# A decoder layer's opening: x's first half loaded early, memory's squares summed by additions, two inverse roots by square root

## The chip, the cores and the metric

The kernel runs on one core of one Trainium2 chip. The metric is the device time of one execution in microseconds; 2423.27 us is the median of the runs before the change.

## The reference

The reference is one layer of a hybrid decoder on 1024 tokens of width 1024. Only its opening matters here.

```python
def rms_norm(x, g):
    xf = x.astype(jnp.float32)
    y = xf * lax.rsqrt(jnp.mean(xf * xf, axis=-1, keepdims=True) + NORM_EPS)
    return (y * g.astype(jnp.float32)).astype(x.dtype)

def swiglu(u, w_in, w_out):
    gate, up = jnp.split(u @ w_in, 2, axis=-1)
    return (jax.nn.silu(gate) * up) @ w_out

# in the layer:
f1 = swiglu(rms_norm(h, ffn1_pre_g[l]), ffn1_w_in[l], ffn1_w_out[l])
...
mem_n = rms_norm(mem, mem_norm_g[l])          # mem: 256 tokens, used by the cross-attention
km, vm = jnp.split(mem_n @ w_kv, 2, axis=-1)  # needs only mem: no result of the layer
```

The rest of the layer (a recurrent branch, a windowed attention, the cross-attention into `mem`, a gated merge and a second SwiGLU) comes after both and is not touched.

## The kernel before

**Layout.** Activations lie feature-major: a tile holds 128 features by 512 tokens. x is 8 feature tiles by two halves of the tokens, `x[k][h]`, 256 KB each; `mem_x` is one tile of 8 by 256 columns. Each float32 operand of a product is split into a rounded part (`hi`, a cast on ACT, L126 for weights, L240 for activations) and a rest (`lo`, a subtraction on DVE, L128 and L241), and a product takes three matmuls, hi by hi, hi by lo, lo by hi (`mm3`, L190 to L192).

**Weights.** They come in strips of 512 KB in one fixed order (`plan`): four strips of memory's key projection (`mkv_k`), four of its value projection (`mkv_v`), then the first feed-forward layer (`ffn1_gate` and so on). `raw` (L113) issues a strip's load on SP's queue into one of two buffers (`RAWS = 2`), so that a third strip's load waits until the first strip has been split. `prefetch` (L155) keeps eight split operands (four strips) ready; it runs inside `take`, before each use. For the `mkv` strips POOL makes the second half's subtraction.

**Order.** The program is written in one order, and a scheduler puts each engine's instructions into theirs: an instruction has the number of its place in the program, and of those that are ready the lowest number goes first. `high_priority(offset=n)` lowers the numbers inside it by n: `lead` is 300, `urgent` is 1000. Each engine then runs its list strictly in order, SP's DMA issues too.

**The opening** (`build`, L1198 to L1205). Memory's two loads are written (`memory_load`, L818), then x's sixteen (L1201), then `memory_kv` (L823), `factors_norm` of x's first half (L288) and `factors_first` (L296).

- `memory_kv`: `mem_hi` and `mem_lo`, memory times its gains, split (L830 on ACT, L831 on DVE). Two halves of squares on ACT (L835, one buffer), each summed over its four feature tiles by one DVE reduction (L837). `rstd` turns the sums into inverse roots. The four `mkv_k` strips are multiplied into four PSUM banks (`pq`); each bank is emptied by L849, which multiplies with the inverse roots (`mem_rs`). The bank tag has four buffers, so `mkv_v`'s two banks wait for L849. Then the four `mkv_v` strips.
- `factors_norm`: squares of the eight x tiles (ACT, L250), seven additions (DVE, L254), `rstd`, then eight multiplications in place (DVE, L294). `factors_first` splits the eight tiles (L240, L241); the first feed-forward products (`px`, `py`) need them.
- `rstd` (L211): matmuls with a column of ones sum over features (`ps_ms`, L218); on DVE, with two or four columns, a scale (L221), a first guess by shifting the bits (L226, L227), and three Newton steps of three instructions (L230 to L232); four matmuls spread the result over the partitions (`ps_rs`, L236). With `quick` the guess is DVE's reciprocal and ScalarE's square root (L223, L224) and one Newton step; before the change only the kernel's last norm, into the output, uses it.

After the opening the feed-forward layer takes nine strips with x's first half alone, while x's second half is loaded, normalized and combined (`factors_part`, `factors_end`), and then goes on with both.

Of the kernel before, what the change touches and what calls it, by code (L numbers as in the profile page):

```python
# [10 lines left out]
F32 = mybir.dt.float32  # L11
F32R = mybir.dt.float32r
I32 = mybir.dt.int32
ALU = mybir.AluOpType
ACT = mybir.ActivationFunctionType
AXX = mybir.AxisListType.X

P = 128
T = 1024
TH = 512  # L20
D = 1024
KD = D // P
DFF = 2816
KF = DFF // P
MEM = 256
# [6 lines left out]
HALVES = ((0, 0, TH), (1, 0, TH))  # L32
# [5 lines left out]
KH = KD // 2  # L38
# [37 lines left out]
class Builder:  # L76
# [208 lines left out]
            self.nc.scalar.copy(raw[:, 8 + h * TH : 8 + (h + 1) * TH], o)  # L285


    def factors_norm(self, xs, part, gname, pool):  # L288

        h, lo, hi = part  # L290
        xs = [x[h][:, lo:hi] for x in xs]
        rs = self.rstd([self.sum_squares(xs, pool)], D, pool, hi - lo)[:, : hi - lo]
        for k in (0, 4, 1, 5, 2, 6, 3, 7):
            self.nc.vector.scalar_tensor_tensor(xs[k], xs[k], self.vec(gname, k), rs, ALU.mult, ALU.mult)  # L294

# [17 lines left out]
    def quarters(self, xs):  # L313
        return ([xs[k + a][h] for k in range(KH)] for h in (0, 1) for a in (0, KH))
# [508 lines left out]
    def memory_kv(self, pool, km_d, vm_d):  # L823
        nc, x = self.nc, self.mem_x
        V = nc.vector
        hi = pool.tile([P, KD, MEM], F32R, name="mem_hi", bufs=1)
        lo = pool.tile([P, KD, MEM], F32R, name="mem_lo", bufs=1)
        for k in range(KD):
            g = self.vec("mem_norm_g", k)
            nc.scalar.activation(hi[:, k], x[:, k], ACT.Copy, scale=g)  # L830
            V.scalar_tensor_tensor(lo[:, k], x[:, k], g, hi[:, k].bitcast(F32), ALU.mult, ALU.subtract)  # L831
        parts = []
        for a in (0, KH):
            sq = pool.tile([P, KH, MEM], F32, tag="mem_sq", name="mem_sq", bufs=1)
            nc.scalar.activation(sq, x[:, a : a + KH], ACT.Square)  # L835
            s = pool.tile([P, MEM], F32, tag="mem_ss", name="mem_ss", bufs=2)
            V.tensor_reduce(s, sq.rearrange("p k t -> p t k"), AXX, ALU.add)  # L837
            parts.append(s)

        ps, col = self.rstd(parts, D, pool, MEM, True)  # L840
        rs = pool.tile([P, MEM], F32, name="mem_rs", bufs=1)
        nc.scalar.copy(rs, ps[:, :MEM])
        for h in range(4):
            w = self.strip("mkv_k", h)
            ps = self.psum("pq")
            for k in range(KD):
                self.mm3(ps[:, :MEM], self.block(w, k), (hi[:, k], lo[:, k]), k == 0, k == KD - 1)
            t = pool.tile([P, MEM], F32, tag="km", name="km", bufs=2)
            V.tensor_tensor(t, ps[:, :MEM], rs, ALU.mult)  # L849
            nc.scalar.dma_start(km_d[:, h], t)  # L850
        pv = [self.psum("pq") for _ in (0, 1)]
        for s in range(4):
            w = [tuple(x.rearrange("p b c -> p (b c)") for x in op) for op in self.strip("mkv_v", s)]
            for a in (0, 1):
                k = 2 * s + a
                for i in (0, 1):
                    cols = slice(i * P, (i + 1) * P)
                    self.mm3(pv[i], (hi[:, k, cols], lo[:, k, cols]), w[a], k == 0, k == KD - 1)
        for i in (0, 1):
            t = pool.tile([P, 512], F32, tag="vm", name="vm", bufs=2)  # L860
            nc.scalar.activation(t, pv[i], ACT.Copy, scale=col[:, i : i + 1])
            nc.scalar.dma_start(vm_d[:, i], t)
# [303 lines left out]
    def build(self):  # L1166
        nc, tc, io = self.nc, self.tc, self.io
        with contextlib.ExitStack() as outer, tc.tile_pool(reuse_waits="tile", name="consts", bufs=1) as cp, \
# [26 lines left out]
            with quarters() as self.qpool:  # L1195
                x = self.acc_tiles()
                with tc.tile_pool(reuse_waits="tile", name="start", bufs=1) as pool:
                    self.memory_load(pool)  # L1198
                    for h in (0, 1):
                        for k in range(KD):  # L1200
                            nc.sync.dma_start(x[k][h], io["xT"][:, k, h * TH : (h + 1) * TH])  # L1201
                    self.memory_kv(pool, km_d, vm_d)
                    self.factors_norm(x, HALVES[0], "ffn1_pre_g", pool)
                    self.factors_first(x)
                self.ffn_in("ffn1", x, hid_d, first_d, HALVES[1:], lambda part, pool: self.factors_norm(x, part, "ffn1_pre_g", pool))  # L1205
                consts, raws = contextlib.ExitStack(), contextlib.ExitStack()
                mixc = consts.enter_context(tc.tile_pool(reuse_waits="tile", name="mixc", bufs=1))
                self.rawpool = raws.enter_context(tc.tile_pool(reuse_waits="tile", name="raws", bufs=len(MIX_FIRST)))
                self.mixer_consts(mixc)
                with tc.tile_pool(reuse_waits="tile", name="ffn_out", bufs=2) as pool:  # L1210
                    acc = self.acc_tiles()
                    for part in self.ffn_outs("ffn1", hid_d, acc, HALVES):
                        xr = self.residual(io["xT"], part, self.res_tile)
                        self.post_norm(acc, part, lambda k: self.post1[:, k : k + 1], xr, pool, h1)
                        self.pre_norm(acc, part, "mix_pre_g", u, pool)
                    self.mixer_first(u, pool, att_d)
            mixed = self.mixer(u, mixc, raws.close, att_d, gate_d, km_d, vm_d)
            consts.close()
            with quarters() as self.qpool:
                merged = self.last_branches(*mixed)  # L1220
                x = self.acc_tiles()
                projection = self.out_projection(merged, x)
                post = lambda part, xr, pool: self.post_norm(x, part, lambda k: self.vec("mix_post_g", k), xr, pool, h2)
                part = next(projection)
# [91 lines left out]
```

## Time and profile before

| | us |
|---|---|
| median of 3 runs (2422.99 to 2425.74) | 2423.27 |
| the profiled execution | 2416.87 |
| its span, first to last instruction | 2415.2 |
| PE busy in the span | 2356.7 |
| DVE busy | 1570.0 |
| ACT busy | 915.2 |
| first product matmul starts, after the span's start | 8.32 |
| first feed-forward matmul starts | 43.81 |

Times inside the execution are counted from the span's start. The profiled execution lies 6.4 us under the median and 1.67 us over its span. PE is TensorE's matmuls, PEld its weight loads, DVE is VectorE, ACT ScalarE, POOL GpSimd, SP the queue that issues most loads (SPq in a row is such an issue, whose duration is that of the issue and not of the transfer). A matmul's duration overlaps its neighbours'; the distance between the starts of two is what one costs.

### The profile page before, as it was taken

The page shows a single profiled execution, that of the slowest core. Times are in us where ns is not written, and L with a number is a line of the kernel's source. Part 1 is how long each engine was busy: PE and PEld are TensorE (multiplying, and loading weights), DVE is VectorE, ACT ScalarE, POOL GpSimd, SP SyncE. Part 2 cuts the span into 40 slices and gives each one's busy share as a digit, 9 for nine tenths or more (in the row PEclk, how much of TensorE's full clock was granted, in tenths as well). Part 3 has the DMA queues.
Part 4 walks back from the last instruction along what each step waited for, and adds up shares of the span by engine and source line. Part 5 has one row for each costly group of instructions (what it writes and reads, how often), then busy time and mean ns, then how long its engine had stood idle before and what let it go on. Part 6 is the DMA issues. An engine that isn't in the chain of part 4 may idle for free.

```text
span 2415.2 us, 33278 instructions
## 1 busy us (share of the span) xinstructions
PE 2356.7 (98%) x12500; PEld 1917.6 (79%) x12500; DVE 1570.0 (65%) x2598; ACT 915.2 (38%) x1712; POOL 105.0 (4%) x142
## 2 busy tenths in 40 slices
PE   7999999999999999999999999999999999999997
PEld 6788888788888777887777877778888778878887
DVE  7976555654488775993435367675988665564457
ACT  6523333422345533222334454334652223342143
POOL 1000000000000000001210000240000000000000
PEclk9999999999999999999999999999999999999999
DMA  7453222532244245225326434454545432253235
GB/s 246 156 187 114 89 86 79 177 117 99 101 157 141 103 149 183 97 96 184 125 78 203 129 114 144 165 181 160 176 162 175 148 127 80 90 197 105 79 112 190
DMA packets 161921, 332.16 MB, mean 138 GB/s; under 512 B 31552, under 2 KB 61760, under 8 KB 161504
## 3 DMA queue, kind: packets, MB, share of 16 engines
q1 hardware_dynamic: 146304, 302.70, 37.1%
q10 hardware_dynamic: 15456, 27.33, 3.2%
q8 instruction: 98, 1.61, 0.3%
q14 instruction: 63, 0.52, 0.1%
HBM read 239.80 MB, written 89.13 MB: 136 GB/s over the span
## 4 chain that ended last, share of the span: by engine, by line
PE 79%; DVE 10%; DMA 5%; ACT 3%; issue 3%; POOL 0%; ACTq 0%; SPq 0%; DVEq 0%; POOLq 0%
PE po L190 6%; PE po L191 6%; PE po L192 6%; PE px L190 5%; PE px L191 5%; PE px L192 5%; PE pgate L190 4%; PE pgate L192 3%; PE pgate L191 3%; PE pz L191 2%; PE pz L192 2%; PE pz L190 2%; DVE w_lo L128 2%; DMA w_raw<-in_ffn_in 2%; PE pr L192 2%
## 5 line engine op out<-in xcount | busy, mean ns | idle before, releaser
L126 ACT CAST w_hi<-w_raw 128x512 fp32r<-128x512 f32 x592 | 363.0, 620 | 883.1 <-PE po L191 260.6
L128 DVE TENSOR_TENSOR w_lo<-w_raw,w_hi 128x512 fp32r<-128x512 f32 x584 | 408.6, 703 | 173.1 <-ACT w_hi L126 166.4
L190 PE MATMUL po<-u,w_hi 128*128 128x512 f32 (+1 forms) x768 | 286.7, 373 | 2.2 <-DVE acc L472 2.2
L192 PE MATMUL po<-u,w_lo 128*128 128x512 f32 (+1 forms) x768 | 286.1, 373 | 0.0
L191 PE MATMUL po<-u,w_hi 128*128 128x512 f32 (+1 forms) x768 | 286.0, 372 | 0.0
L475 DVE TENSOR_TENSOR acc<-po,acc 128x512 f32<-128x512 f32 (+1 forms) x136 | 89.5, 658 | 154.4 <-PE po L192 154.1
L190 PEld LDWEIGHTS po<-u,w_hi 128*128 128x128 f32 x768 | 145.4, 189 | 28.1 <-DVE acc L472 3.4
L192 PEld LDWEIGHTS po<-u,w_lo 128*128 128x128 f32 x768 | 145.5, 189 | 25.1
L191 PEld LDWEIGHTS po<-u,w_hi 128*128 128x128 f32 x768 | 145.4, 189 | 24.8
L190 PE MATMUL pgate<-u,w_hi 128*128 128x512 f32 x384 | 154.2, 402 | 0.0
L192 PE MATMUL pgate<-u,w_lo 128*128 128x512 f32 x384 | 153.7, 400 | 0.0
L191 PE MATMUL pgate<-u,w_hi 128*128 128x512 f32 x384 | 153.0, 399 | 0.0
L190 PE MATMUL px<-f,w_hi 128*128 128x512 f32 x352 | 137.9, 392 | 6.2 <-DVE u L396 4.2
L191 PE MATMUL px<-u,w_hi 128*128 128x512 f32 x352 | 137.3, 390 | 0.6 <-DVE u L241 0.6
L191 PE MATMUL pz<-u,w_hi 128*128 128x512 f32 x352 | 136.9, 389 | 0.3 <-DVE u L241 0.3
L190 PE MATMUL px<-u,w_hi 128*128 128x512 f32 x352 | 136.9, 389 | 0.3 <-ACT u L240 0.3
L192 PE MATMUL px<-u,w_lo 128*128 128x512 f32 x352 | 137.2, 390 | 0.0
L191 PE MATMUL px<-f,w_hi 128*128 128x512 f32 x352 | 137.1, 389 | 0.0
L192 PE MATMUL px<-f,w_lo 128*128 128x512 f32 x352 | 137.1, 389 | 0.0
L192 PE MATMUL pz<-u,w_lo 128*128 128x512 f32 x352 | 136.9, 389 | 0.0
L190 PE MATMUL pz<-u,w_hi 128*128 128x512 f32 x352 | 136.9, 389 | 0.0
L192 PE MATMUL pr<-u,w_lo 128*128 128x512 f32 x224 | 89.1, 398 | 0.0
(324 smaller groups left out, 4679.2 us busy)
## 6 DMA issues: line engine op xcount, KB each, us to landing
w_raw<-in_ffn_in SPq DMA_DIRECT2D x110, 512.0 KB
w_raw<-in_ffn_out SPq DMA_DIRECT2D x68, 512.0 KB
w_raw<-in_win SPq DMA_DIRECT2D x56, 512.0 KB
hid_d<-g SPq DMA_DIRECT2D x88, 256.0 KB
hid<-hid_d SPq DMA_DIRECT2D x88, 256.0 KB
gate_d<-gate SPq DMA_DIRECT2D x24, 512.0 KB
pk_d<-pk ACTq DMA_DIRECT2D x4, 2560.0 KB
f<-pk_d SPq DMA_DIRECT2D x16, 640.0 KB
```

The source lines that it names most:

```text
L126: self.nc.scalar.copy(hi, x)
L128: (engine or self.nc.vector).tensor_tensor(lo, x, hi.bitcast(F32), ALU.subtract)
L190: mm(out, wh, xh, start=first, stop=False, **kw)
L191: mm(out, wh, xl, start=False, stop=False, **kw)
L192: mm(out, wl, xh, start=False, stop=last, **kw)
L475: self.nc.vector.tensor_tensor(out, ps, out, ALU.add)
```

## The change

`rstd`'s `quick` is handed through `factors_norm`; the function itself is as before. `prefetch` is called ahead of everything else, x's first half is loaded with numbers lowered by 1000, and x's second half is loaded after `memory_kv` in the program. Memory's two halves of squares get a buffer each; one addition of 128x1024 adds them, and two more (128x512 and 128x256) fold the four tiles that are left, so that `ps_ms` takes one operand in place of two.

```diff
-    def factors_norm(self, xs, part, gname, pool):
+    def factors_norm(self, xs, part, gname, pool, quick=False):
...
-        rs = self.rstd([self.sum_squares(xs, pool)], D, pool, hi - lo)[:, : hi - lo]
+        rs = self.rstd([self.sum_squares(xs, pool)], D, pool, hi - lo, quick=quick)[:, : hi - lo]
...
-        parts = []
+        sqs = []
         for a in (0, KH):
-            sq = pool.tile([P, KH, MEM], F32, tag="mem_sq", name="mem_sq", bufs=1)
+            sq = pool.tile([P, KH, MEM], F32, tag="mem_sq", name="mem_sq", bufs=2)
             nc.scalar.activation(sq, x[:, a : a + KH], ACT.Square)
-            s = pool.tile([P, MEM], F32, tag="mem_ss", name="mem_ss", bufs=2)
-            V.tensor_reduce(s, sq.rearrange("p k t -> p t k"), AXX, ALU.add)
-            parts.append(s)
-
-        ps, col = self.rstd(parts, D, pool, MEM, True)
+            sqs.append(sq)
+        s = sqs[0]
+        V.tensor_tensor(s, s, sqs[1], ALU.add)
+        for n in (2, 1):
+            V.tensor_tensor(s[:, :n], s[:, :n], s[:, n : 2 * n], ALU.add)
+
+        ps, col = self.rstd([s[:, 0]], D, pool, MEM, True, quick=True)
...
+                    self.prefetch()
                     self.memory_load(pool)
-                    for h in (0, 1):
-                        for k in range(KD):
-                            nc.sync.dma_start(x[k][h], io["xT"][:, k, h * TH : (h + 1) * TH])
+                    load = lambda h: [nc.sync.dma_start(x[k][h], io["xT"][:, k, h * TH : (h + 1) * TH]) for k in range(KD)]
+                    with tc.high_priority(offset=self.urgent):
+                        load(0)
                     self.memory_kv(pool, km_d, vm_d)
-                    self.factors_norm(x, HALVES[0], "ffn1_pre_g", pool)
+                    load(1)
+                    self.factors_norm(x, HALVES[0], "ffn1_pre_g", pool, quick=True)
```

## Rows read from the trace of the kernel before

**Rows 1.** The page, busy time of each engine (us, share of the span, instructions)

```profile
PE 2356.7 (98%) x12500; PEld 1917.6 (79%) x12500; DVE 1570.0 (65%) x2598; ACT 915.2 (38%) x1712; POOL 105.0 (4%) x142
```

**Rows 2.** Busy time by stretches: PE, PEld, DVE, ACT, POOL, granted clock, DMA share, GB/s

```profile
8.00:14.00 6.00, 5.68 (x25) 5.49 (x26) 5.38 (x10) 5.56 (x12) 1.04 (x2) 1.00 1.01 383
27.90:34.50 6.60, 6.60 (x20) 5.54 (x21) 4.67 (x17) 1.88 (x4) 2.54 (x2) 0.50 0.84 277
43.80:48.70 4.90, 3.67 (x14) 1.94 (x12) 4.41 (x8) 3.70 (x8) 0.00 (x0) 1.00 0.73 222
70.00:100.00 30.00, 30.00 (x134) 24.84 (x133) 29.05 (x48) 15.67 (x28) 0.00 (x0) 1.00 0.50 167
```

**Rows 3.** PE in order of time: start, duration, line, operation, idle before and its releaser

```profile
8.32 0.79 PE L190 MATMUL pq<-mem_hi,w_hi 128*128 128x256 f32 x2 [8.32 <-ACT mem_hi L830]
...
26.49 0.71 PE L236 MATMUL ps_rs<-ident,rsy 128*128 128x128 f32 x4 [2.44 <-DVE rsy L232]
27.89 1.87 PE L218 MATMUL ps_ms<-ones,sq 128*128 128x1 f32 x8 [0.69 <-DVE sq L254]
...
31.04 0.63 PE L190 MATMUL pq<-w_hi,mem_hi 128*128 128x512 f32 x1
31.47 0.63 PE L191 MATMUL pq<-w_lo,mem_hi 128*128 128x512 f32 x1
...
34.96 1.05 PE L236 MATMUL ps_rs<-ident,rsy 128*128 128x128 f32 x8
...
43.81 0.39 PE L190 MATMUL px<-u,w_hi 128*128 128x512 f32 x1
44.04 0.39 PE L190 MATMUL py<-r,w_hi 128*128 128x512 f32 x1
...
62.29 1.02 PE L218 MATMUL ps_ms<-ones,sq 128*128 128x1 f32 x8 [1.08 <-DVE sq L254]
...
104.60 0.50 PE L191 MATMUL pz<-u,w_hi 128*128 128x512 f32 x1 [0.34 <-DVE u L241]
```

**Rows 4.** SP's queue in order of time, its first issues

```profile
0.81 0.87 SPq L119 DMA_DIRECT2D w_raw<-in_mkv_k  x2
1.73 0.90 SPq L821 DMA_DIRECT2D mem_x<-in_memT  x2
2.67 1.06 SPq L1201 DMA_DIRECT2D acc<-in_xT  x2
7.03 2.00 SPq L119 DMA_DIRECT2D w_raw<-in_mkv_k  x2
```

**Rows 5.** The chain of waits in order of time: start, length, what

```profile
1.73 5.95 DMA mem_x<-in_memT
```

**Rows 6.** DVE in order of time, memory's squares and inverse root

```profile
15.40 2.03 DVE L837 TENSOR_REDUCE mem_ss<-mem_sq 128x256 f32<-128x1024 f32 x1
...
18.35 0.16 DVE L221 TENSOR_SCALAR rsm<-ps_ms 128x2 f32<-128x2 f32 x1 [0.26 <-PE ps_ms L218]
...
21.29 1.26 DVE L231 TENSOR_TENSOR rsq<-rsq,rsh 128x2 f32<-128x2 f32 x1
...
22.86 0.68 DVE L254 TENSOR_TENSOR sq<-sq 128x512 f32<-128x512 f32 x1
...
26.27 0.16 DVE L232 SCALAR_TENSOR_TENSOR rsy<-rsq,rsy 128x2 f32<-128x2 f32 x1
```

**Rows 7.** POOL in order of time

```profile
16.24 1.29 POOL L128 TENSOR_TENSOR w_lo<-w_raw,w_hi 128x512 fp32r<-128x512 f32 x1 [1.31 <-ACT w_hi L126]
20.88 1.66 POOL L128 TENSOR_TENSOR w_lo<-w_raw,w_hi 128x512 fp32r<-128x512 f32 x1 [3.34 <-ACT w_hi L126]
```

**Rows 8.** The kernel's end, ACT's table load, then the chain of waits

```profile
2352.56 1.28 ACT L224 ACT_TABLE_LOAD   x1
...
2404.99 0.17 DVE rsm L221
...
2406.01 0.17 DVE rsy L232
```

## The prediction, made before the changed kernel was run

> **What bounds the kernel now.** The page's busy times come first [rows 1]: PE is busy 2356.7 of 2415.2 us, no other engine over 65%. So the kernel is as long as TensorE's work plus the time in which TensorE stands still or runs slowly, and an opening can give only the second kind. The busy times by stretches show where in the opening that is [rows 2]: 27.9 to 34.5 us runs at a granted clock of 0.50, and from 43.8 to 48.7 us PE is busy for 3.67 of 4.90 us. PE in order of time names the waits [rows 3]. It starts at 8.32 us, when memory's first split tile is there; it waits 2.44 us for memory's inverse roots (the `mkv_v` products need a PSUM bank, a bank is emptied by L849, and L849 needs the roots); then 0.69 us for the sum of x's squares; and it comes back to the `mkv_v` products at half clock, 0.43 us from one matmul to the next against 0.23 us for the same width at 43.81. The chain of waits begins with memory's own load, 1.73 to 7.68 us [rows 5]. So early on two things bound: when memory arrives, and DVE's chain from memory and x to their roots. Later there is a second bound: from 70 to 100 us DVE is busy 29.05 of 30 us, and at 104.60 a matmul waits 0.34 us for DVE's split of x's second half [rows 2, 3]. What the opening gains must be gained on DVE too, or it is lost there.
>
> **x's loads.** The code lowers their numbers by 1000, the weights' by 300. That numbers decide, and not the place in the program, is seen on SP's queue: the first two strips are written after memory and x, and are issued first, at 0.81, with memory at 1.73 and x at 2.67 [rows 4]. The third strip waits for its buffer until 7.03. Ahead of it now stand all eight x tiles, which is what the change says. But memory's loads have no lowered number, so I take it that x goes ahead of memory as well (and probably of the first two strips, which changes nothing in the sum). That is 8 tiles of 256 KB, 2.10 MB. When the queues are full the transfers run at 383 GB/s from 8 to 14 us [rows 2], so memory lands 5.5 us later, near 13.2 us, and PE's first product starts near 13.8. Cost: **+5.5**. The other end is 0, memory still first. SP's issues themselves cost little: two x issues took 1.06 us [rows 4], eight take 4.2, inside that time. Third and fourth strip come about 3 us later than now, behind 1.05 MB of memory; PE has two strips to work on by then, and I cost them at 0. If that cover is gone, it is at most the same 5.5.
>
> **What then leaves PE's path.** (a) x's sum and root. x is in by about 8 us (5.5 us of transfer from 2.7 on), its squares need ACT and DVE, which have little else to do before memory comes; so `ps_ms` (1.87 us) and `ps_rs` (1.05 us) [rows 3] run while PE has nothing to do: **-2.9**. The wait of 0.69 goes with them: **-0.7**. (b) Memory's root. Today it takes from 18.35 to 26.43 (26.27 and 0.16), 8.1 us, since its 12 small instructions after L221 stand between 0.68 us additions and w_lo subtractions on DVE, and one of them took 1.26 us [rows 6]. The quick form stands at the kernel's end: from L221 to the last step 1.2 us where nothing lies between [rows 8]. In company I take 3 us; the bounds are 1.2 and 8.1. The squares' sums cost two reductions of 2.03 us [rows 6]; the three additions, by 0.68 for 512 columns, 1.4 + 0.7 + 0.4 = 2.5 us, so 1.5 us less. The chain from memory's landing to the roots was 26.43 - 7.68 = 18.75 us and becomes about 12; PE asks for the roots at 26.49 - 2.44 = 24.05, 15.7 us after its start, and so finds them with 3 us to spare: **-2.4**. (c) One operand in place of two in `ps_ms` takes out two of its four products; I take **-0.4** (0 to 0.9, from half of 1.87). (d) Without the idle time ahead of them, the `mkv_v` products run at full clock. From 29.6 to 34.5 us 12 of them came 0.43 apart in place of 0.23: **-2.4**, or 0 if the clock falls all the same. (e) From 43.8 to 48.7 us 14 matmuls need 3.2 us at 0.23 and take 4.9; they wait for splits of x [rows 2, 3] which DVE will have made: **-1.7**, or 0 where the splits stay last. (f) The wait of 1.08 us ahead of the second half's `ps_ms` at 62.29 goes in part: **-0.5** (0 to -1.1).
>
> ScalarE gets two square roots and at most one more load of its tables, 1.28 us at the kernel's end [rows 8]; both lie in the 3 us to spare in (b). x's second half is now written after `memory_kv`, as filler for SP behind the strips; its sum is asked for only at 62.29 [rows 3], and nine strips of the first half alone cover it: 0, or a later wait there if it lands late.
>
> Sum: +5.5 - 2.9 - 0.7 - 2.4 - 0.4 - 2.4 - 1.7 - 0.5 = **-5.5 us**. On DVE the same stretch loses 1.5 us of sums, seven small instructions of 0.16 us in each of two roots (2.2), and some of the waits like that of 1.26 us (three L231 took 1.2 us or more; one shows in rows 6): 3.7 to 7 us; and it has idle time to give, 1.9 us in 27.9 to 34.5 alone. So DVE can just follow by 5.5 us and the gain can be kept. Against the profiled execution, 2416.87 us, this gives 2411.4; the median stands 6.4 above that execution, so the forecast is 2423.27 - 5.5, or **2417.8**.
>
> **A rule against it.** Memory's reduction at 15.40 took 2.03 us although POOL's subtraction ran from 16.24 to 17.53 beside it; L231, with two operands in SBUF, began at 21.29 inside POOL's 20.88 to 22.54 and ended with it [rows 6, 7]. The additions have two such operands, so by POOL's durations one of them can wait 0 to 1.7 us. Two such waits, 3.4 us, would use up the 3 us to spare in (b) and cost PE 0.4: a sum of -5.1 in place of -5.5, or 2418.2. I take none, since POOL works less than half of that stretch. The Trainium skill's page "SBUF — State Buffer" (Who interferes with whom) has it as a rule: a DVE instruction with two SBUF inputs and a GpSimd one that reads SBUF block each other whole, and a reduction never contends. The trace agrees.
>
> **The rivals.** *Memory is not behind x* (SP takes the strips and memory first, as the words "ahead of the third strip" may mean). For it: that is what they say; against it: the numbers. Then the +5.5 falls away, but x's matmuls stay on the path, +2.9, and DVE, which could follow by 7 to 9 at most, bounds: about -8.5, **2414.8**. *The gain is given back*: the opening is shorter, but DVE at 100 us has not followed, or the strips' loads come late. For it: DVE is full in that stretch; against it: its removed work. By DVE's lower figure, 3.7, less one POOL wait of 1.7, the gain is about 2: **2421.3**. *Memory's late arrival decides*: the stretch from memory to the first feed-forward product keeps its length, because L849 still waits for the roots behind DVE's x work (eight multiplications and seven additions now stand ready just when memory comes), PE idles and the clock falls as before. Then only the +5.5 is left: **2428.8**, slower. It decides if the wait ahead of `ps_rs` stays over 2 us; against it is that the small root's instructions are fewer and go first by number. The half-way case, stalls half gone, lies within 0.2%.
>
> **The numbers.** 0.2% is 4.85 us, about what a measurement can tell. Chances: the forecast 0.50, its own range 2415.5 to 2420.0; memory first 0.15; given back 0.23; memory late 0.12. Faster by over 0.2% (under 2418.4) is memory first and seven tenths of the forecast's own range, 0.51; within 0.2% is the rest of it and the gain given back, 0.37; slower is 0.12. The range from 2413.8 to 2425.5 leaves out most of the slower case and the best of memory first.
>
> **What would show it.** On SP's queue eight x issues before memory's, memory landing near 13 us and the first product near 13.8; x's `ps_ms` and `ps_rs` before that product; no wait over 0.5 us ahead of memory's `ps_rs`; a granted clock of 1.00 through the `mkv_v` products; the first feed-forward product near 40 us with no gaps after it; and the strips after 100 us still some 5 us earlier. A wait of 2 us or more for roots, a clock of 0.50 after it, or a wait at x's second half that grows by what the opening gained would prove the sum wrong, each at its own term.

## The result: slower by a quarter of a per cent

The changed kernel took 2432.94 us (median of 15 runs, 2429.27 to 2436.60), the kernel before beside it 2427.17 us (15 runs): a ratio of 1.0026, with a 95% interval of [1.0018, 1.0035]. Run a second time (after_again, below), the change gave 1.0036 [1.0024, 1.0048]. That is slower by more than the 0.2% that the prediction took for measurable (the lower end of the first interval lies a little under it), where it had forecast 5.5 us faster.

| | before, us | after, us |
|---|---|---|
| profiled execution | 2416.87 | 2429.78 |
| its span | 2415.2 | 2428.1 |
| first product matmul starts | 8.32 | 14.20 |
| memory's `ps_rs` starts | 26.49 | 29.69 |
| first `mkv_v` matmul starts | 29.62 | 31.68 |
| x's `ps_ms` starts | 27.89 | 42.59 |
| first feed-forward matmul starts | 43.81 | 50.85 |
| first store of a hidden tile (L415) | 124.21 | 132.07 |

The spans differ by 12.9 us, the medians by 5.8. A second profile of the kernel before, below, has a span of 2422.2 with an opening like the first one's; so two profiles of one kernel differ by 7 us, and only the opening is compared row by row here, never the two spans.

The page's busy times after answer to [rows 1]: PE is as busy as before, within 1.0 us, so the time that was added is time in which PE stands still.

```profile
PE 2357.7 (97%) x12496; PEld 1918.5 (79%) x12496; DVE 1564.8 (64%) x2585; ACT 917.2 (38%) x1715; POOL 107.5 (4%) x142
```

SP's queue after, in order of time, against [rows 4]:

```profile
0.81 3.90 SPq L1203 DMA_DIRECT2D acc<-in_xT  x8
4.75 0.91 SPq L119 DMA_DIRECT2D w_raw<-in_mkv_k  x2
5.70 1.25 SPq L821 DMA_DIRECT2D mem_x<-in_memT  x2
```

All eight x loads stand ahead of everything, memory included.

PE after, in order of time, against [rows 3] (start, duration, line, operation, idle before and its releaser):

```profile
14.20 0.80 PE L190 MATMUL pq<-mem_hi,w_hi 128*128 128x256 f32 x2 [14.20 <-ACT mem_hi L830]
...
29.69 0.71 PE L236 MATMUL ps_rs<-ident,rsy 128*128 128x128 f32 x4 [1.37 <-DVE rsy L232]
...
31.68 0.40 PE L190 MATMUL pq<-w_hi,mem_hi 128*128 128x512 f32 x1
31.91 0.40 PE L191 MATMUL pq<-w_lo,mem_hi 128*128 128x512 f32 x1
...
42.59 0.95 PE L218 MATMUL ps_ms<-ones,sq 128*128 128x1 f32 x8
46.63 1.16 PE L236 MATMUL ps_rs<-ident,rsy 128*128 128x128 f32 x8 [3.10 <-DVE rsy L232]
50.85 0.79 PE L190 MATMUL px<-u,w_hi 128*128 128x512 f32 x1 [3.07 <-ACT u L240]
...
55.41 0.80 PE L191 MATMUL px<-u,w_hi 128*128 128x512 f32 x1 [2.25 <-DVE u L241]
56.01 0.63 PE L192 MATMUL px<-u,w_lo 128*128 128x512 f32 x1
56.43 0.63 PE L190 MATMUL px<-u,w_hi 128*128 128x512 f32 x1
```

The first `mkv_v` matmul of the kernel before, a row that [rows 3] leaves out, is:

```profile
29.62 0.77 PE L190 MATMUL pq<-w_hi,mem_hi 128*128 128x512 f32 x1
```

So the `mkv_v` products begin 2.1 us later than before (31.68), although memory's first product began 5.9 us later, and they run at full pace, 0.23 from one to the next. When the last is out, at 42.59, PE stands 1.2 us earlier than where the kernel before began its feed-forward products. But here x's `ps_ms` comes behind the last `mkv_v` product, where it came ahead of the first one before. What hangs on it then runs one step after the other with PE waiting: root (3.10), `ps_rs`, multiplications and splits (3.07 and 2.25). From 42.59 to 50.85 there are 8.3 us with 2.1 us of work in them (0.95 and 1.16).

Busy time by stretches after, against [rows 2] (PE, PEld, DVE, ACT, POOL, granted clock, DMA share, GB/s):

```profile
27.90:34.50 6.60, 5.23 (x33) 4.54 (x32) 2.29 (x7) 3.16 (x6) 2.31 (x2) 1.00 0.51 158
...
43.80:48.70 4.90, 1.16 (x8) 0.97 (x8) 2.43 (x8) 2.40 (x6) 0.00 (x0) 0.92 0.81 229
48.70:60.80 12.10, 7.70 (x17) 5.24 (x18) 12.06 (x20) 7.20 (x14) 0.00 (x0) 0.50 0.23 81
```

The stretch at a granted clock of 0.50 has not gone; it has moved from 27.9 to 34.5 us to behind the new idle time. From 48.7 to 60.8 PE is at the lower of its two levels, 0.43 us from one product to the next, and up to 55.41 DVE, busy for 12.06 of 12.10 us, is what holds it: it waits for DVE's splits and, through ACT's casts, for DVE's multiplications.

DVE after, in order of time, against [rows 6]:

```profile
8.25 3.08 DVE L254 TENSOR_TENSOR sq<-sq 128x512 f32<-128x512 f32 x4 [0.38 <-ACT sq L250]
...
25.86 0.16 DVE L221 TENSOR_SCALAR rsm<-ps_ms 128x2 f32<-128x2 f32 x1 [1.11 <-PE ps_ms L218]
...
29.47 0.16 DVE L232 SCALAR_TENSOR_TENSOR rsy<-rsq,rsy 128x2 f32<-128x2 f32 x1
...
48.20 1.29 DVE L128 TENSOR_TENSOR w_lo<-w_raw,w_hi 128x512 fp32r<-128x512 f32 x2 [1.63 <-ACT w_hi L126]
49.41 5.35 DVE L294 SCALAR_TENSOR_TENSOR acc<-acc,vecs,ps_rs 128x512 f32<-128x512 f32 x8
54.67 0.68 DVE L241 TENSOR_TENSOR u<-acc,u 128x512 fp32r<-128x512 f32 x1
```

x's last addition ends at 11.33 us (8.25 and 3.08): the sum lies ready 31 us before PE takes it. Before, the eight multiplications were spread under the `mkv_v` products (from 36.05 to 44.64); now they come in one piece, from 49.41.

The chain of waits after, from 43.75 (start, length, what), shows what the multiplications stood behind:

```profile
43.75 3.77 DMA w_raw<-in_ffn_in
...
47.55 0.63 ACT w_hi L126
...
48.20 1.29 DVE w_lo L128 x2
49.49 2.63 DVE acc L294 x4
```

DVE's list runs strictly in order, and in it two subtractions of a weight strip stand between the root and the multiplications; that strip lands only at 47.5.

### The profile page after: what moved, and what is told of

Same layout as the page of the kernel before. It is cut to its first block, busy times and chain, and to the rows that moved or that the text cites. A ratio compares the mean times of both kernels' runs of the same rounds, so it can differ in the third digit from the quotient of the medians.

```text
span 2428.1 us, 33264 instructions
## 1 busy us (share of the span) xinstructions
PE 2357.7 (97%) x12496; PEld 1918.5 (79%) x12496; DVE 1564.8 (64%) x2585; ACT 917.2 (38%) x1715; POOL 107.5 (4%) x142
## 4 chain that ended last, share of the span: by engine, by line
PE 76%; DVE 11%; DMA 7%; issue 3%; ACT 3%; POOL 0%; SPq 0%; ACTq 0%; DVEq 0%; POOLq 0%
PE po L190 6%; PE po L191 6%; PE po L192 6%; PE px L191 5%; PE px L190 5%; PE px L192 5%; PE pgate L190 3%; PE pgate L192 3%; PE pgate L191 3%; DMA w_raw<-in_ffn_in 3%; DVE w_lo L128 3%; PE pz L190 2%; PE pz L191 2%; PE pz L192 2%; PE pr L192 2%
```

## Experiments

Two theories stood against each other. **Order**: the loss is that x's `ps_ms` has its place on PE behind the last `mkv_v` product. **Memory late**: the loss is the 5.9 us by which memory's products start later, the one rival on the slower side. Ratios are to the kernel before, run beside each kernel on its chip.

| kernel | us, median | ratio [95%] |
|---|---|---|
| load_only | 2436.68 | 1.0066 [1.0051, 1.0082] |
| quick_only | 2426.22 | 1.0025 [1.0013, 1.0037] |
| sums_only | 2423.47 | 1.0014 [1.0002, 1.0025] |
| after_sum_early | 2423.51 | 1.0018 [1.0008, 1.0028] |
| (before, beside these four) | 2419.80 | |
| after_again | 2434.32 | 1.0036 [1.0024, 1.0048] |
| mem_then_x | 2434.07 | 1.0036 [1.0023, 1.0050] |
| mem_then_x_sum_early | 2424.50 | 0.9996 [0.9987, 1.0005] |
| mem_then_x_sum_early_table | 2460.37 | 1.0145 [1.0127, 1.0163] |
| (before, beside these four) | 2426.14 | |
| mtx_early_table2 | 2424.78 | 1.0000 [0.9988, 1.0011] |
| pad_only | 2460.99 | 1.0152 [1.0136, 1.0168] |
| quick_sum_early | 2428.22 | 1.0012 [1.0003, 1.0021] |
| mtx_early_reduce | 2428.56 | 1.0015 [1.0006, 1.0024] |
| (before, beside these four) | 2425.52 | |
| before_again | 2424.47 | 0.9996 [0.9987, 1.0006] |
| after_sum_early_b | 2429.31 | 1.0018 [1.0008, 1.0028] |
| mtx_sum_early_b | 2426.48 | 0.9996 [0.9986, 1.0005] |
| mem_first_sum_early_table2 | 2425.82 | 1.0002 [0.9992, 1.0012] |
| (before, beside these four) | 2426.82 | |

### The parts alone

**load_only**: the kernel before with the new order of loads alone.

```diff
+                    self.prefetch()
                     self.memory_load(pool)
...
+                    with tc.high_priority(offset=self.urgent):
+                        load(0)
                     self.memory_kv(pool, km_d, vm_d)
+                    load(1)
```

> The kernel before with the changed order of loads alone (x's first half ahead of everything). Theory 1, TensorE's order: x's ps_ms has a later number than memory's products and stands behind the last mkv_v product, so that x's root, its eight multiplications and the first splits run after it with TensorE idle; x's ps_ms starts over 42 us although its sum is ready near 11 us, the first px matmul starts over 50 us, and the time is 6 to 12 us above the kernel before. Theory 2, memory late: memory's load behind x costs its 5.5 to 6 us and nothing else; x's ps_ms comes before the first mkv product or between k and v, the first px matmul near 49 us, the time 4 to 6 us above before.

It was the worst of the parts, 1.0066, some 16 us: more than either theory had expected. PE in order of time, of load_only:

```profile
43.45 0.95 PE L218 MATMUL ps_ms<-ones,sq 128*128 128x1 f32 x8
51.40 2.07 PE L236 MATMUL ps_rs<-ident,rsy 128*128 128x128 f32 x8 [7.00 <-DVE rsy L232]
```

x's `ps_ms` is behind the `mkv_v` products here too, and with the long root the wait behind it is 7.00 us where the changed kernel has 3.10.

**quick_only**: the quick root alone, for memory and for x's first half.

```diff
-        ps, col = self.rstd(parts, D, pool, MEM, True)
+        ps, col = self.rstd(parts, D, pool, MEM, True, quick=True)
...
-                    self.factors_norm(x, HALVES[0], "ffn1_pre_g", pool)
+                    self.factors_norm(x, HALVES[0], "ffn1_pre_g", pool, quick=True)
```

> The kernel before with the two quick roots alone; memory is loaded first, as before. Theory 1 (order): memory's root no longer holds TensorE, so x's ps_ms loses its place between the k and the v products and goes behind v: first product at 8.3 us as before, ps_ms of x at 37 to 39 us, first px matmul at 44 to 46 us, the feed-forward products come in at half clock after the idle time, and the time is 0 to 5 us above the kernel before. Theory 2 (memory late): nothing that costs is in this kernel, so it is 3 to 5 us faster than before.

1.0025, some 6 us, a little over what order had expected. Memory's `ps_rs` comes 2.4 us earlier than before (24.05 against 26.49), but x's `ps_ms` has moved from ahead of the `mkv_v` products to behind them (39.18), and PE waits 2.55, 1.49, 2.32 and 2.67 us in what follows. So a shorter root alone makes the kernel slower, and either of the two parts moves x's sum.

**sums_only**: the three additions alone.

```diff
-            s = pool.tile([P, MEM], F32, tag="mem_ss", name="mem_ss", bufs=2)
-            V.tensor_reduce(s, sq.rearrange("p k t -> p t k"), AXX, ALU.add)
-            parts.append(s)
+            sqs.append(sq)
+        s = sqs[0]
+        V.tensor_tensor(s, s, sqs[1], ALU.add)
+        for n in (2, 1):
+            V.tensor_tensor(s[:, :n], s[:, :n], s[:, n : 2 * n], ALU.add)
```

> The kernel before with memory's squares summed by three additions alone. Both theories: memory's sum is there 1 to 3 us earlier, x's ps_ms keeps its place between the k and the v products, the time is 0 to 3 us below the kernel before. If the additions wait for POOL's subtractions (over 3 us for the three together), the time is that of before within 1 us.

A miss: 1.0014, slower, with x's `ps_ms` in its old place (28.46). Memory's `ps_ms` came at 18.86 against 17.48 before. DVE in order of time, of sums_only:

```profile
13.13 1.22 DVE L838 TENSOR_TENSOR mem_sq<-mem_sq 128x1024 f32<-128x1024 f32 x1 [1.41 <-ACT mem_sq L835]
14.27 3.47 DVE L128 TENSOR_TENSOR w_lo<-w_raw,w_hi 128x512 fp32r<-128x512 f32 x2
17.67 1.14 DVE L840 TENSOR_TENSOR mem_sq<-mem_sq 128x512 f32<-128x512 f32 x2
```

And POOL in order of time, of sums_only:

```profile
14.20 2.99 POOL L128 TENSOR_TENSOR w_lo<-w_raw,w_hi 128x512 fp32r<-128x512 f32 x2 [5.64 <-ACT w_hi L126]
```

The additions themselves are as short as the prediction had them (1.22 and 1.14 us). But two strip subtractions stand between the first and the second, and these took 3.47 us (14.27 to 17.74) beside POOL's 14.20 to 17.19, where two of them take 1.29 (48.20 in the changed kernel): 2.2 us more. The Trainium skill's page "SBUF — State Buffer" (Who interferes with whom) has it that a DVE instruction with two SBUF inputs contends with a GpSimd instruction that reads SBUF, and that the later of the two is blocked whole; the trace agrees, though the instruction that was shut out is not the one that was added.

**after_sum_early**: the changed kernel with the numbers of x's `ps_ms` lowered by 1000, nothing else.

```diff
-        for j in range(nb):
-            for i, sq in enumerate(sqs):
-                nc.tensor.matmul(ps[:, j : j + 1], ...)
+        with self.tc.high_priority(offset=early) if early else contextlib.nullcontext():
+            for j in range(nb):
+                for i, sq in enumerate(sqs):
+                    nc.tensor.matmul(ps[:, j : j + 1], ...)
```

> The changed kernel with one thing more: the four ps_ms products of x's first half get numbers lowered by 1000, so that TensorE takes them as soon as the sum is there by the scheduler's reckoning. Theory 1 (order): ps_ms of x by 30 us, the multiplications of x on VectorE under the v products, the first px matmul right behind the last v product near 45 us at full clock, the first store of a gate product 8 to 11 us earlier than in the changed kernel, the time 8 to 11 us below the changed kernel and 1 to 4 us below the kernel before. Theory 2 (memory late): the 5.5 to 6 us stay, so the time falls by less than 3 us and stays 3 us or more above the kernel before.

PE in order of time, of after_sum_early:

```profile
28.58 0.95 PE L219 MATMUL ps_ms<-ones,sq 128*128 128x1 f32 x8
...
43.15 0.39 PE L190 MATMUL px<-u,w_hi 128*128 128x512 f32 x1
45.56 0.50 PE L191 MATMUL px<-u,w_hi 128*128 128x512 f32 x1 [1.79 <-DVE u L242]
```

x's sum goes ahead of the `mkv_v` products, the first feed-forward matmul starts at 43.15 in place of 50.85, and the store of the first hidden tile at 125.48 in place of 132.07. The trace does what order expected; the time does not: 1.0018 here and again on another chip, 4.4 us above the kernel before, is nearer to what memory late had expected. It lies under the change's 1.0026 and 1.0036, but the intervals overlap and the two never ran side by side. So order is not the whole loss.

x's sum does not go ahead of memory's first product, though, which starts at 14.03 here: even with numbers lowered by 1000 its place in PE's list is 17 us after the sum is ready (DVE's last addition ends at 11.27). Why the scheduler puts it there is not shown.

### Memory ahead of x

**after_again**: the changed kernel once more, beside the next three.

> The changed kernel itself, on the chip of the three others. Every theory: its ratio to the kernel before was 1.0026, so 4 to 9 us above before; ps_ms of x's first half again behind the last mkv_v product, at 42 to 43 us.

1.0036; PE has x's `ps_ms` at 41.94 and the first feed-forward matmul at 51.03, as in the first profile.

**mem_then_x**: the changed kernel, but SP issues two strips and memory first, then x's first half, then the third strip.

```diff
+                    with tc.high_priority(offset=3000):
+                        self.load_strips(2)
+                    with tc.high_priority(offset=2000):
+                        self.memory_load(pool)
                     self.prefetch()
-                    self.memory_load(pool)
```

(`load_strips` issues the first two strips' loads as `raw` does.)

> The changed kernel with two strips and memory loaded first, then x's first half, then the third strip. Memory lands near 7.7 us as in the kernel before. Theory 1 (TensorE's order): the first product starts near 8.4 us and the last mkv_v product ends near 37 us, 5.8 us earlier than in the changed kernel, but x's ps_ms stands still behind it, so that some 12 us of idle time and half clock follow as in the changed kernel: first px matmul at 44 to 46 us, time 5 to 7 us below the changed kernel, within 2 us of the kernel before. Theory 2 (memory late is the loss): nothing else costs, so 3 to 6 us below the kernel before.

PE in order of time, of mem_then_x:

```profile
8.72 0.79 PE L197 MATMUL pq<-mem_hi,w_hi 128*128 128x256 f32 x2 [8.72 <-ACT mem_hi L837]
...
18.59 0.52 PE L197 MATMUL pq<-mem_hi,w_hi 128*128 128x256 f32 x1 [1.17 <-ACT w_hi L133]
...
39.72 0.95 PE L225 MATMUL ps_ms<-ones,sq 128*128 128x1 f32 x8
44.73 2.07 PE L243 MATMUL ps_rs<-ident,rsy 128*128 128x128 f32 x8 [4.06 <-DVE rsy L239]
49.86 0.80 PE L197 MATMUL px<-u,w_hi 128*128 128x512 f32 x1 [3.06 <-ACT u L247]
```

Memory is back at 8.72, and the time is the same, 1.0036 beside after_again's 1.0036. As the whole cause, memory late falls. But the 5 to 7 us less that order had expected did not come either. Where the 5.5 us went: x's sum is still behind the `mkv_v` products, and what follows waits for the same strip as in the changed kernel. DVE in order of time, of mem_then_x:

```profile
48.28 1.29 DVE L135 TENSOR_TENSOR w_lo<-w_raw,w_hi 128x512 fp32r<-128x512 f32 x2 [0.69 <-ACT w_hi L133]
49.49 2.71 DVE L301 SCALAR_TENSOR_TENSOR acc<-acc,vecs,ps_rs 128x512 f32<-128x512 f32 x4
```

All but one of the multiplications start at 49.49, behind the subtractions at 48.28, against 49.41 and 48.20 above. With x's sum late, the pace of the strips sets the first feed-forward product, whatever memory does. (That is read from the rows; no run moved that strip alone.)

**mem_then_x_sum_early**: mem_then_x with the edit of after_sum_early, the lowered numbers of x's `ps_ms`.

> The same, and x's ps_ms with numbers lowered by 1000. Theory 1: ps_ms of x by 25 us, first px matmul at 37 to 40 us at full clock; the gate products come 4 to 6 us earlier than in the kernel before, and as far as VectorE can follow after 100 us, the time is 3 to 6 us below the kernel before and another 4 to 6 us below the kernel with memory first alone. Theory 2: within 1.5 us of the kernel with memory first alone.

PE in order of time, of mem_then_x_sum_early:

```profile
26.04 0.98 PE L226 MATMUL ps_ms<-ones,sq 128*128 128x1 f32 x8
...
41.28 0.39 PE L197 MATMUL px<-u,w_hi 128*128 128x512 f32 x1
```

0.9996 [0.9987, 1.0005]: all of the loss is gone, though the 3 to 6 us below the kernel before that order had expected are not there. Against mem_then_x, on the same chip, the numbers of eight small matmuls are worth 2434.07 - 2424.50 = 9.6 us. This is the run that decides: order is a cause, where memory is early. With after_sum_early it gives the other one its place:

| | x's sum behind the `mkv_v` products | x's sum ahead of them |
|---|---|---|
| memory behind x | 1.0026 and 1.0036 (the change) | 1.0018 and 1.0018 |
| memory ahead of x | 1.0036 | 0.9996 and 0.9996 |

Memory late costs nothing while x's sum is late, and 0.22% (5.3 us) once it isn't; x's sum late costs 0.40% with memory early, and 0.08 to 0.18% with memory late, which overlapping intervals leave open. Either is enough to make the kernel slower; the two hide each other.

**mem_then_x_sum_early_table**: the same, and ScalarE's square root table loaded at the start, by a square root into a new tile of one column.

```diff
+            warm = cp.tile([P, 1], F32, name="warm")
+            nc.scalar.activation(warm, self.ones, ACT.Sqrt)
             self.ident = cp.tile([P, P], F32, name="ident")
```

> The same again, with a square root of one column as ScalarE's first instruction, so that its table is the one loaded at the start. The load of 1.28 us ahead of memory's root goes; both theories: 0 to 1.5 us below the kernel without it.

A miss by 34 us: 1.0145, and not in the opening. The next two runs took it apart.

### The table and the tile

**mtx_early_table2**: the early square root written into a tile that exists and is overwritten after it.

```diff
+            nc.scalar.activation(self.post1[:, :1], self.ones, ACT.Sqrt)
             nc.vector.tensor_scalar(self.post1, self.vecs...
```

> Memory first, then x, x's ps_ms early, and ScalarE's first instruction a square root, as in the kernel that came out 1.45% slower, but the root is written into a tile that is there already (the first column of the halved gains, written over afterwards), so that no tile moves in SBUF. Theory A: that kernel was slow since one more 128x1 tile moved the tiles behind it and each 512-column matmul took 0.233 us in place of 0.227; then the distance here is 0.227 again and the time 0 to 2 us below the kernel without the root, so 0 to 3 us below the kernel before. Theory B: the square root's table itself slows what follows; then 30 us above before again.

1.0000 [0.9988, 1.0011]: the table is loaded at 1.25 us and not again ahead of memory's root, and the time is that of mem_then_x_sum_early. So the table load costs nothing that the time shows, and the 34 us were not the table.

**pad_only**: the kernel before with one more tile of one column, set once and never read.

```diff
+            pad = cp.tile([P, 1], F32, name="pad")
+            nc.vector.memset(pad, 1.0)
             self.ident = cp.tile([P, P], F32, name="ident")
```

> The kernel before with one tile of 128x1 more and a memset of it, nothing else. Theory A (place in SBUF): the 512-column matmuls come 0.233 us apart in place of 0.227 and the time is 25 to 40 us above before. Theory B (table): 0.227 us, time that of before within 3 us.

1.0152 [1.0136, 1.0168], 35 us from a tile of 512 bytes. PE in order of time, of pad_only:

```profile
299.98 0.40 PE L190 MATMUL pz<-u,w_hi 128*128 128x512 f32 x1
...
300.68 0.40 PE L190 MATMUL px<-f,w_hi 128*128 128x512 f32 x1
```

And the kernel before at the same place:

```profile
299.87 0.39 PE L190 MATMUL px<-u,w_hi 128*128 128x512 f32 x1
...
300.55 0.39 PE L190 MATMUL px<-u,w_hi 128*128 128x512 f32 x1
```

From the first row of each to the second are three matmuls: 0.70 us there, 0.68 here, at a granted clock of 1.00 in both (250 to 350 us). mem_then_x_sum_early_table has the longer distance too (299.80, 300.03, 300.26, 300.50); all the other kernels of this study have the shorter, so none of their comparisons rests on this.

### What is left of each part when the order is right

**quick_sum_early**: quick_only with x's `ps_ms` lowered.

> The kernel before with the two quick roots, and x's ps_ms with numbers lowered by 1000; loads and sums as before. Theory 1 (TensorE's order made the quick roots slower): ps_ms of x at 27 to 31 us under the v products in place of 39 us, first px matmul at 39 to 42 us at full clock, time 4 to 8 us below the kernel with the quick roots alone, 0 to 3 us below before. If the order was not it: within 2 us of the kernel with the quick roots alone, 5 to 7 us above before.

1.0012 against quick_only's 1.0025, on different chips: the first hidden store moves from 129.7 to 125.9, the time by 0.13%, with intervals that overlap. The quick root with the right order still gains nothing over the kernel before: at 48.08 PE waits 3.11 us for a split of x.

**mtx_early_reduce**: mem_then_x_sum_early with the two reductions put back in place of the additions.

> The kernel with memory first, then x, and x's ps_ms early, whose memory squares are summed by the two reductions again. If the additions cost (they wait for POOL's subtractions, and sums alone came out 0.14% slower): 0 to 4 us below the kernel with the additions. If they gain by their fewer columns: 1 to 3 us above it, with ps_ms of memory 1 to 2 us later than 16.2 us.

1.0015 [1.0006, 1.0024], where the additions gave 0.9996 (and 1.0000 beside it, with the early table): memory's `ps_ms` is at 17.53 in place of 16.23. So the additions, which alone cost 0.14%, gain 0.15 to 0.19% in this company. That this hangs on what stands between them on DVE, as in sums_only, is likely but not shown.

### Again, and the best of it

**before_again**, **after_sum_early_b** and **mtx_sum_early_b** are the kernel before, after_sum_early and mem_then_x_sum_early once more, on one chip.

> The kernel before, profiled once more. Its first profile lay 6.4 us under the median. Every theory: time that of before within 1 us. In the trace the opening repeats (first px matmul 43.5 to 44.5 us, first store of the hidden values at 124 to 125 us, the first product of the layer's output at 478 to 480 us); if the span is 4 to 8 us longer, the difference comes after that, and only the opening's places in the traces may be compared, not the spans.

> The changed kernel with x's ps_ms early, again, on the chip of the next one. Memory lands 5.5 us later than in the next one. If memory's late arrival still costs once TensorE's order is right (theory 2 as a second term), 4 to 6 us above the next kernel; if the third and fourth strip, which come later in the next one, give it back (TensorE waits for them and falls to half clock), within 3 us of it. Against before: ratio 1.001 to 1.003, as measured.

> Memory first, then x, x's ps_ms early, again: ratio to before 0.999 to 1.0005, as measured; first px matmul 41 to 42 us; a wait for the third strip's split of 1 us or more near 18 us and half clock after it.

The kernel before against itself gave 0.9996 [0.9987, 1.0006], its profile a span of 2422.2 against 2415.2 in the first, with the first feed-forward matmul at 43.37 (43.81) and the first hidden store at 125.4 (124.2). The other two repeated their ratios to the last digit, 1.0018 and 0.9996: the 0.22% between memory late and memory early stands on both pairs. On this chip, where the two ran side by side, their medians differ by 2.8 us, so its size in us is known only roughly. Their traces repeat less well: the first feed-forward matmul is at 44.33 and 42.81 (43.15 and 41.28 in the first profiles) and the first hidden store at 127.6 and 124.4 (125.5 and 122.7). So a difference of 1 to 2 us between two single traces shows nothing by itself.

**mem_first_sum_early_table2**: memory and all the strips of the first `prefetch` ahead of x, x's `ps_ms` lowered, the table loaded at the start; all that was learnt in one kernel.

```diff
-                    self.prefetch()
-                    self.memory_load(pool)
+                    with tc.high_priority(offset=3000):
+                        self.prefetch()
+                    with tc.high_priority(offset=2000):
+                        self.memory_load(pool)
```

> The three parts with the loads in the order of the kernel before (memory first, the third strip not behind x), x's ps_ms early and the square root's table loaded at the start. No wait for the third strip near 18 us; if the strip's wait and the half clock after it were what the former kernel gave back, first px matmul at 39 to 41 us and 1 to 4 us below before; if VectorE after 100 us is what gives it back, within 1.5 us of before, with waits for L396's additions of 2 to 4 us between 100 and 480 us.

1.0002 [0.9992, 1.0012]. Its first feed-forward matmul is at 40.07, 3.3 us ahead of before_again's 43.37, and the first hidden store 1.9 ahead (123.5 against 125.4). From 60 to 480 us the longest line in the table of PE's waits (us in total, times, longest us) is this one:

```profile
PE px L190 <- DVE u L397: 3.8, 3, 1.5
```

In before_again, on the same chip, the same line of the program (its L396) has as much:

```profile
PE px L190 <- DVE u L396: 3.6, 5, 1.5
```

So DVE's waits do not show the gain given back there. At the first output tile (L472, here L473) this kernel is still 1.7 us ahead (480.4 against 482.1); the 5.3 us by which its span is longer come after that, where nothing of the program was changed and two profiles of the kernel before differ too. A lead of 1.7 us is 0.07% and lies inside the interval, so the runs tell neither that it is kept nor that it is lost. The third strip's wait is gone, but not the half clock: PE waits 1.51 us for memory's sum at 18.94, and from 19 to 23 us the granted clock is 0.58. No version beat the kernel before by more than its interval.

## Why the prediction was wrong

**The step that failed is (a)**: that x's `ps_ms` and `ps_rs` "run while PE has nothing to do", -2.9, with the wait of 0.69 gone too. The reason given was true: x was in, squared and summed by 11.33 us, and PE had nothing to do until 14.20. What was left out is the order of PE's list. The prediction looked at whose data are ready, and at numbers only for SP's queue; x's `ps_ms` has a later number than all of memory's products, and nothing lowers it (`rstd` lowers the steps behind it, `ps_rs` among them, but not `ps_ms`). In place of 3.6 us less, x's sum came 31 us after it was ready, and PE had 2.1 us of work in the 8.3 us behind the last `mkv_v` product. The place that it had before, between the `mkv_k` and the `mkv_v` products [rows 3], came from the stall for memory's root: no `mkv_v` product had a bank, so x's sum was the lowest number that could go. The change shortens that stall, and with it the place is gone. That the list was made so is shown (the lowered numbers bring it back, at 28.58 and 26.04, and with memory early are worth 9.6 us); that it is the scheduler's own reckoning of the shorter stall that does it is argued, from load_only and quick_only, which both move the sum and both bring memory's root nearer to its products, and sums_only, which does neither. On the chip PE still had 1.37 us free ahead of memory's `ps_rs`.

(a) is not the whole of the miss. The prediction's gains come to 11.0 us, beside the +5.5. With x's sum ahead of the `mkv_v` products the kernel is still 0.18%, 4.4 us, slower, so that some 1 us of gains is left beside the +5.5; with memory early as well the kernel is 1 us faster, inside its interval. The other terms were too large too, as the next paragraphs show for (b) and (e); how the 10 us divide among them is not shown.

**+5.5 for x's loads** was right as a time (x goes ahead of memory; 14.20 against the 13.8 worked out), and right as a price where nothing else is late: 0.22%, 5.3 us, with x's sum ahead. In the changed kernel it cost nothing (mem_then_x); by the rows, because the strip at 47.5 us was later still.

**(b)** was too good. The larger part lies ahead of the root: from memory's first product to the root's first step it was 10.0 us before (8.32 to 18.35) and is 11.7 now (14.20 to 25.86), where the prediction took 1.5 off. The root itself took from 25.86 to 29.63, 3.8 us against the 3 assumed, since ScalarE runs its list in order too: a strip's cast, which waited 2.36 us for PE and started at 26.91, and then the table load stand ahead of its square root. ACT after, in order of time:

```profile
26.91 0.62 ACT L126 CAST w_hi<-w_raw 128x512 fp32r<-128x512 f32 x1 [2.36 <-PE pq L192]
27.55 1.28 ACT L224 ACT_TABLE_LOAD   x1
28.85 0.20 ACT L224 ACTIVATE rsy<-rsy 128x2 f32<-128x2 f32 x1
```

The prediction put the 1.28 us into 3 us of spare time (4.2 by its own figures: roots 11.5 us after the first product, asked for 15.7 after it). It was not there: the roots came 15.4 us after the first product, and PE waited 1.37 of its former 2.44. The Trainium skill's page "ScalarE: Activation LUTs" (What ACT_TABLE_LOAD costs) gives 2.66 us for a switch, a drain included; here the cast ended at 27.53 and the root began at 28.85, so 1.3 us is all of it.

**(d)** was right: the `mkv_v` products ran at a granted clock of 1.00. The half clock came later, behind the idle time of (a), from 48.7 to 60.8. **(e)** went the other way: in place of 1.7 us less, waits of 3.07 and 2.25 us for x's splits, since all eight multiplications and the splits behind them now start at 49.41. With x's sum ahead (after_sum_early) PE still waits 1.79 us for a split, at 45.56. **(c)** came as it was put: memory's `ps_ms` is four rows in place of eight (x2 and x6 before); its 0.4 us can't be told apart in the time. **(f)**: the second half's `ps_ms` (69.29) no longer waits, but it comes 7.0 us later than before.

**The rule about POOL** was weighed at its price of 3.4 us but on the wrong instruction: sums_only shows 2.2 us lost by the subtractions between the additions, and there the time is 0.14% longer. In the changed kernel the first addition took 1.47 us (at 21.36) against 1.22, so the additions themselves lost about 0.3 us.

**The rival "memory's late arrival decides"** named the time well (5.5 us slower; 5.8 by the medians) and not the mechanism. It wanted a wait of over 2 us ahead of memory's `ps_rs`, with x's work ahead of memory's roots on DVE, and a low clock in the `mkv_v` products; the wait was 1.37, x's additions were done at 11.33, and the clock was full. Taken away (mem_then_x), the late arrival gave back nothing. **Memory not behind x**, 2414.8 or -8.5, is mem_then_x with the right order: 0.9996, about -1 us, so that sum was far too large as well. The rows show one reason: the third strip is now behind x, PE waits 1.15 us for its cast, and from 21 to 26 us runs at a granted clock of 0.50. But mem_first_sum_early_table2, without that wait, is not measurably faster, so the reason stays open. So does the **gain given back**, the rival with 0.23: a lead of 1.7 us stands at 480 us, and the time can't tell what becomes of it.

## What to carry to other kernels

A stall on an engine that runs its list in order is also the place where other work got done; before removing one, look which instructions stand in it, and where the scheduler puts them when it is gone. If the first link of a chain keeps its late place, lowering the rest of the chain's numbers gains nothing: give the whole chain one rank, above all its few cheap instructions on the busiest engine. Two faults that each make a stretch long can hide each other, so undo them one at a time and together. And compare a trace with the nearest profile of the kernel before, or with two: one of them waited 1.4 us at a line where the other waited 3.6.

## What was not expected of the hardware

One more tile of 128x1 made 512-column matmuls slower by about 3% (0.70 us for three against 0.68) and the kernel by 1.52% [1.36, 1.68]. The tile holds 4 bytes in each partition, so it can move every tile placed after it; that the place of the operands in SBUF is the cause fits the two kernels that had such a tile, but which place costs what was not tried. And two profiles of one kernel differed by 7 us in span, more than most of the effects here, with nearly the same opening: at this size only the timed pairs decide, and a trace says where, not how much. Even the first hidden store moved by up to 2.1 us between two profiles of one kernel.
